# Gate and up products of a 512-token SwiGLU half step by seven half-size products, their weight sums and part of adaLN on GpSimd

## The chip, the cores and the metric

The kernel runs on one NeuronCore of a Trainium2 chip. The metric is device time in microseconds for one launch. In the profile the engines are PE (TensorE, with its weight loads as PEld), DVE (VectorE), ACT (ScalarE), POOL (GpSimd) and SP (SyncE, which issues most DMAs). SBUF is the on-chip memory and PSUM the accumulators that PE writes.

## The reference

Two transformer layers over 256 latent and 256 context tokens, 1024 features, everything in float32. Each layer has a SwiGLU half step, a token mixer with four kinds of attention, and a second SwiGLU half step; all three start from an RMS norm whose scale and shift (and the gate of the result) come from adaLN, a product of a condition vector with `w_ada`. Latent and context tokens have different condition vectors. In the last layer only latent tokens go past the mixer. Cut to the part that matters here:

```python
for l in range(2):
    mod   = (silu(c)     @ w_ada[l] + b_ada[l]).reshape(B, 9, 1, D)   # latent
    mod_c = (silu(c_ctx) @ w_ada[l] + b_ada[l]).reshape(9, D)         # context
    h  = h  + 0.5 * mod[:, 2] * swiglu(modulate(h,  norm_ffn1[l], mod[:, 0], mod[:, 1]), w_gu, w_down)
    hc = hc + 0.5 * mod_c[2]  * swiglu(modulate(hc, norm_ffn1[l], mod_c[0], mod_c[1]), w_gu, w_down)
    ...  # token mixer
    h  = h + 0.5 * mod[:, 8] * swiglu(...)          # and hc in the first layer only
# swiglu(u) = (silu(u @ w_gate) * (u @ w_up)) @ w_down, w_gate and w_up 1024 x 2816
```

## The kernel before

Activations lie feature-major: a tile has 128 features on the partitions and up to 512 tokens along it, tokens 0 to 255 latent (`LAT`), 256 to 511 context (`CTX`). Every float32 operand of a large product is split into a high part in the PE's fast format (`fp32r`) and the rest (`lo`): ACT casts the high part (L127), DVE subtracts it from the raw tile (L128), and `mm3` (L132) issues three matmuls, high x high, high x low and low x high. A weight block is 128 x 1024 (8 contraction tiles `k` of 128 x 128), DMA'd by SP into one of three raw buffers (`wraw`) and split into one of five `whi`/`wlo` pairs (`weights`, L119).

A half step is `ffn` (L350). Its 22 tiles of 128 hidden features come in chunks of 8, 8 and 6 (`FF_CHUNKS`). For a tile j, `pair(j)` (L375) loads and splits a gate block and an up block, 2 x 8 x 3 matmuls of 512 columns sum into two PSUM banks, and `activate` (L353) takes silu of gate on ACT, multiplies by up on DVE (L358) and splits the result into `ah`/`al` (L371, L372). After a chunk the eight down tiles follow: for output tile m, 8 (or 6) x 3 matmuls over the chunk's activations, and DVE adds the result with its gate into the residual stream `h` (L336). The last five down tiles of a half step run for one half of the tokens after the other (matmuls of 256 columns), woven with the next norm. The first two tiles of a half step are done k by k behind the norm that makes `u`, the normed operand (`first_products`, L264, or `first_opening`, L987, in the first half step). The second half step of layer 2 has 256 tokens only.

adaLN's vectors other than the first two are computed beside the half steps: `Jobs` (L315) hands out tiles at a fixed rate, `jobs.run(2)` after a gate/up tile and `jobs.run(1)` after a down tile. A tile (`ada_tile`, L292) is a 128 x 1024 block of `w_ada` DMA'd into `wa`, and two DVE instructions (L298) that multiply it with the latent and the context condition vector and add up along the row. The first half step has 48 such tiles, the second 32, the third (layer 2, first) 48.

The code is written in the order of the data flow. A planner with its own estimates of the instructions' costs orders each engine's queue from it and places every wait; `keep_in_program_order` fixes single instructions (here adaLN's products and the opening's matmuls). On the chip each engine takes its queue in order.

Of the kernel before, what the change touches and what calls it, by code (L numbers as in the profile page):

```python
# [49 lines left out]
def body(nc, tc, es, a):  # L50
# [47 lines left out]
    def late_constants():  # L98
        """-lam per layer, on every partition; rev"""
# [31 lines left out]

    def mm3(ps, lw, rw, start, stop, pin=False):  # L132
        (lh, ll), (rh, rl) = lw, rw
        ins = nc.tensor.matmul(ps, lh, rh, start=start, stop=False)  # L134
        if pin:
            tc.keep_in_program_order(ins)
        nc.tensor.matmul(ps, lh, rl, start=False, stop=False)  # L137
        nc.tensor.matmul(ps, ll, rh, start=False, stop=stop)  # L138
# [1062 lines left out]
```

## Time and profile before

| what | value |
|---|---|
| timed runs, median (lowest to highest) | 2156.77 us (2156.07 to 2157.89) |
| profiled execution, span from first to last instruction | 2153.2 us |
| PE busy | 2107.4 us (98%) |
| DVE busy | 1469.2 us (68%) |
| ACT busy | 911.8 us (42%) |
| POOL busy | 180.7 us (8%) |
| mean granted PE clock (1 is 2.4 GHz) | 0.997 |

For the profiled execution the page gives the span; the timed runs are 3.6 us above it in the median. Busy time is the share of the span in which an engine works on an instruction. A record of a DVE or POOL instruction runs from its start to its end and includes any time in which it is held inside; two instructions in a row on an engine overlap by a little, so what one costs in a dense stretch is read from start to start. Matmuls overlap more: 512 columns are recorded with 0.39 us but follow each other at a shorter distance.

### The profile page before, as it was taken

How to read it: one execution, taken by the hardware profiler on the slowest of the kernel's cores; microseconds unless marked ns; L12 is line 12 of the kernel's file. 1: busy time of each engine (PE TensorE's matmuls, PEld its weight loads, DVE VectorE, ACT ScalarE, POOL GpSimd, SP SyncE). 2: the span in 40 equal slices, each digit the busy share in tenths (PEclk: the TensorE clock that was granted, in tenths of full speed). 3: DMA queues.
4: the chain of work that ended last, by engine and by line, in shares of the span. 5: the costliest groups of instructions: out<-in, count | busy, mean ns of one | idle time of the engine just before them, and what ended most of it. 6: DMA issues, size and time to landing. Idle time of an engine off the chain costs nothing.

```text
span 2153.2 us, 31572 instructions
## 1 busy us (share of the span) xinstructions
PE 2107.4 (98%) x12130; PEld 1805.8 (84%) x12130; DVE 1469.2 (68%) x2639; ACT 911.8 (42%) x1456; POOL 180.7 (8%) x322
## 2 busy tenths in 40 slices
PE   7999999999999999999999999999999999999998
PEld 5888888987777877988888898888889888999998
DVE  6776767678767665566665558767667887787655
ACT  3422222467655563432222233222225776765443
POOL 0000000110012112100000010000002433120000
PEclk9999999999999999999999999999999999999999
DMA  8555554241232223245444336555542335355553
GB/s 331 173 178 178 177 176 150 69 121 47 66 100 73 88 66 118 92 157 156 140 154 150 105 118 203 179 176 186 165 127 90 105 106 138 128 168 171 192 183 102
DMA packets 95207, 301.52 MB, mean 140 GB/s; under 512 B 18640, under 2 KB 20048, under 8 KB 94672
## 3 DMA queue, kind: packets, MB, share of 16 engines
q1 hardware_dynamic: 92080, 295.10, 43.0%
q0 software_dynamic: 2688, 4.20, 1.0%
q8 instruction: 96, 1.57, 0.3%
q14 instruction: 55, 0.45, 0.1%
q10 hardware_dynamic: 288, 0.20, 0.0%
HBM read 294.21 MB, written 1.05 MB: 137 GB/s over the span
## 4 chain that ended last, share of the span: by engine, by line
PE 89%; DVE 5%; ACT 2%; issue 1%; POOL 1%; DMA 1%; SPq 0%; DVEq 0%; POOLq 0%; ACTq 0%
PE pgu L134 13%; PE pgu L137 13%; PE pgu L138 13%; PE pd L137 6%; PE pd L138 6%; PE pd L134 6%; PE pgt L134 4%; PE pgt L137 4%; PE pgt L138 4%; PE av L789 2%; PE pj L134 2%; PE pj L137 2%; PE pj L138 2%; PE psS L735 2%; PE tps L775 1%
## 5 line engine op out<-in xcount | busy, mean ns | idle before, releaser
L127 ACT CAST whi<-wraw 128x1024 fp32r<-128x1024 f32 (+2 forms) x414 | 423.1, 1024 | 993.8 <-PE pgu L137 434.7
L128 DVE TENSOR_TENSOR wlo<-wraw,whi 128x1024 fp32r<-128x1024 f32 (+2 forms) x414 | 495.2, 1197 | 160.6 <-ACT whi L127 141.5
L134 PE MATMUL pgu<-uh,whi 128*128 128x512 f32 (+1 forms) x1440 | 511.9, 357 | 1.4 <-ACT sg L357 0.9
L137 PE MATMUL pgu<-ul,whi 128*128 128x512 f32 (+1 forms) x1440 | 512.7, 356 | 0.6 <-DVE ul L230 0.4
L138 PE MATMUL pgu<-uh,wlo 128*128 128x512 f32 (+1 forms) x1440 | 512.2, 356 | 0.0
L298 DVE SCALAR_TENSOR_TENSOR junk<-wa,sbc 128x1024 f32<-128x1024 f32 x256 | 312.3, 1220 | 3.1
L134 PEld LDWEIGHTS pgu<-uh,whi 128*128 128x128 f32 x1440 | 271.1, 189 | 43.4 <-issue 2.5
L137 PEld LDWEIGHTS pgu<-ul,whi 128*128 128x128 f32 x1440 | 272.1, 189 | 39.4 <-DVE ul L230 1.1
L138 PEld LDWEIGHTS pgu<-uh,wlo 128*128 128x128 f32 x1440 | 272.1, 189 | 39.1 <-DVE wlo L128 0.3
L137 PE MATMUL pd<-al,whi 128*128 128x512 f32 (+1 forms) x794 | 273.4, 344 | 0.2 <-DVE al L372 0.2
L134 PE MATMUL pd<-ah,whi 128*128 128x512 f32 (+1 forms) x794 | 273.5, 345 | 0.0
L138 PE MATMUL pd<-ah,wlo 128*128 128x512 f32 (+1 forms) x794 | 273.1, 344 | 0.0
L134 PE MATMUL pgt<-uh,whi 128*128 128x512 f32 (+1 forms) x512 | 176.5, 345 | 0.4 <-ACT cacc L548 0.4
L358 DVE TENSOR_TENSOR af<-sg,pgu 128x512 f32<-128x512 f32 (+1 forms) x86 | 53.6, 625 | 179.5 <-PE pgu L138 179.5
L137 PE MATMUL pgt<-ul,whi 128*128 128x512 f32 (+1 forms) x512 | 174.1, 340 | 0.0
L138 PE MATMUL pgt<-uh,wlo 128*128 128x512 f32 (+1 forms) x512 | 173.8, 339 | 0.0
L137 PEld LDWEIGHTS pd<-al,whi 128*128 128x128 f32 x794 | 149.3, 188 | 20.9 <-DVE al L372 0.9
L134 PEld LDWEIGHTS pd<-ah,whi 128*128 128x128 f32 x794 | 149.2, 188 | 20.0
L138 PEld LDWEIGHTS pd<-ah,wlo 128*128 128x128 f32 x794 | 149.1, 188 | 19.9
L336 DVE SCALAR_TENSOR_TENSOR h<-pd,mod,h 128x256 f32<-128x256 f32 x168 | 76.4, 480 | 105.7 <-PE pd L138 105.3
L148 POOL TENSOR_TENSOR rq<-ry 128x2 f32<-128x2 f32 (+2 forms) x48 | 12.1, 252 | 1252.5 <-DVE ry L146 1241.6
L134 PEld LDWEIGHTS pgt<-uh,whi 128*128 128x128 f32 x512 | 97.6, 191 | 13.2 <-issue 3.3
(240 smaller groups left out, 3125.2 us busy)
## 6 DMA issues: line engine op xcount, KB each, us to landing
wraw<-wgu SPq DMA_DIRECT2D x176, 512.0 KB, 3.3
wa<-wada SPq DMA_DIRECT2D x128, 512.0 KB, 4.2
wraw<-wd SPq DMA_DIRECT2D x64, 512.0 KB, 3.6
wraw<-wgate SPq DMA_DIRECT2D x64, 512.0 KB, 3.3
wraw<-win SPq DMA_DIRECT2D x28, 512.0 KB, 3.3
wraw<-wd SPq DMA_DIRECT2D x32, 384.0 KB, 3.1
w<-wada SPq DMA_DIRECT2D x16, 512.0 KB, 8.0
wraw<-wbr SPq DMA_DIRECT2D x16, 512.0 KB, 3.3
```

The costliest lines, as they stand in the source:

```text
L127: nc.scalar.copy(hi[:, :n], raw[:, :n])
L128: nc.vector.tensor_sub(lo[:, :n], raw[:, :n], hi[:, :n])
L134: ins = nc.tensor.matmul(ps, lh, rh, start=start, stop=False)
L137: nc.tensor.matmul(ps, lh, rl, start=False, stop=False)
L138: nc.tensor.matmul(ps, ll, rh, start=False, stop=stop)
L148: eng.tensor_mul(q[:, :n], y[:, :n], y[:, :n])
L298: ins = nc.vector.scalar_tensor_tensor(junk, w, 1.0, sbc[:, v], op0=ALU.mult, op1=ALU.mult, accum_out=m[:, t, v:v + 1])
L336: nc.vector.scalar_tensor_tensor(h[k][:, hv[0]:hv[1]], ps[:, off:off + S], gate[:, k, v:v + 1], h[k][:, hv[0]:hv[1]], op0=ALU.mult, op1=AL ...
L358: nc.vector.tensor_mul(af[:, :ntok], sg[:, :ntok], pu[:, :ntok])
L735: nc.tensor.matmul(ps[:, :nk], q_[:, q0:q0 + P], k_[:, self.k0:T], start=z == 0, stop=z == len(qs) - 1 and not bias_mm)
L775: nc.tensor.transpose(tps[:, b], self.p[:, b * P:(b + 1) * P], ident)
L789: nc.tensor.matmul(av[un.qt * 64:(un.qt + 1) * 64], V[br](u0.k0 // P + b, hd), un.pT[:, b], start=b == 0, stop=b == kt - 1)
```

## The change

The gate/up products of the tiles j from 3 on (from 4 on in the first half step) in the three half steps with 512 tokens are done by one level of Strassen's scheme in Winograd's form. The 2 x 2 block matrix of weights is (gate, up) by (k 0 to 3, k 4 to 7), that of the operand is (k 0 to 3, k 4 to 7) by (latent, context). Seven products of 4 x 3 matmuls with 256 columns take the place of eight. `combine` forms the operand's sums T1 to T4 once per half step (each split again into high and low; T4 overwrites the context half of `u`), beside the last plain tile. `seven(j)` forms four weight sums of 128 x 512 per tile on GpSimd, partly in place in the raw tiles, splits the results (`x2`, `x3`, `x1`, beside `xg`, the gate block itself), and adds the products up with five DVE sums of 256 columns. adaLN's context product moves to GpSimd (`tensor_mul` into the `wa` tile), its row sum to ACT one step later; tiles of which only the latent vector is used (layer 2, from vector 5 on) have one product. The rates of `Jobs`, some buffer counts (a fourth raw buffer for odd j, `ah`/`al` 8 for 10, `af` 2 for 3) and tags change. Comments of the code are dropped as well. The core of the diff:

```diff
-    def weights(src, shape):
-        """load a [128, k, cols] block of a weight and split it"""
+    def load(src, shape, pool=None):
         n = shape[1] * shape[2]
-        raw = wp.tile([P, 1024], F32, name="wraw", tag="wraw", bufs=3)
-        rv = raw[:, :n].rearrange("p (k c) -> p k c", k=shape[1])
-        nc.sync.dma_start(rv, src)
+        raw = (pool or wp).tile([P, 1024], F32, name="wraw", tag="wraw", bufs=1 if pool else 3)
+        nc.sync.dma_start(raw[:, :n].rearrange("p (k c) -> p k c", k=shape[1]), src)
+        return raw[:, :n]
+    def split(raw, k):
+        n = raw.shape[1]
         hi = wp.tile([P, 1024], F32R, name="whi", tag="whi")
         lo = wp.tile([P, 1024], F32R, name="wlo", tag="wlo")
-        nc.scalar.copy(hi[:, :n], raw[:, :n])
-        nc.vector.tensor_sub(lo[:, :n], raw[:, :n], hi[:, :n])
-        return (hi[:, :n].rearrange("p (k c) -> p k c", k=shape[1]),
-                lo[:, :n].rearrange("p (k c) -> p k c", k=shape[1]))
-    def mm3(ps, lw, rw, start, stop, pin=False):
+        nc.scalar.copy(hi[:, :n], raw)
+        nc.vector.tensor_sub(lo[:, :n], raw, hi[:, :n])
+        return (hi[:, :n].rearrange("p (k c) -> p k c", k=k), lo[:, :n].rearrange("p (k c) -> p k c", k=k))
+    def weights(src, shape):
+        return split(load(src, shape), shape[1])
...
+    def ada_vectors(l, i):
+        return 1 if l == DEPTH - 1 and i > 4 else 2
-        for v in range(2):
-            junk = pool.tile([P, D], F32, name="junk", tag="junk", bufs=1)
-            ins = nc.vector.scalar_tensor_tensor(junk, w, 1.0, sbc[:, v], op0=ALU.mult, op1=ALU.mult, accum_out=m[:, t, v:v + 1])
-            if pin:
-                tc.keep_in_program_order(ins)
+        junk = pool.tile([P, D], F32, name="junk", tag="junk", bufs=1)
+        ins = nc.vector.scalar_tensor_tensor(junk, w, 1.0, sbc[:, 0], op0=ALU.mult, op1=ALU.mult, accum_out=m[:, t, 0:1])
+        if pin:
+            tc.keep_in_program_order(ins)
+        if ada_vectors(l, i) == 1:
+            return None
+        nc.gpsimd.tensor_mul(w, w, sbc[:, 1])
+        def total():
+            tc.keep_in_program_order(nc.scalar.activation(w, w, AF.Copy, accum_out=m[:, t, 1:2]))
+        return total
...
+        def __init__(self, todo, pool, steps):
+            self.todo, self.rate, self.due, self.pool = todo, len(todo) / steps, 0.0, pool
+            self.sbc, self.n, self.behind = None, 0, []
+            self.need = KD if todo and todo[0][1] in (2, 8) else 0
+        def first(self, n):
+            while self.n < n and self.todo:
+                self.run(0 if self.due >= 1 else 1 / self.rate)
+        def settle(self):
+            for f in self.behind:
+                f()
+            self.behind = []
+        def run(self, steps):
+            self.due += steps * self.rate
+            self.settle()
...
-                ada_tile(l, i, t, self.pool, self.sbc, self.n < PIN)
+                total = ada_tile(l, i, t, self.pool, self.sbc, self.n < PIN)
                 self.n += 1
                 if t == KD - 1:
+                    self.settle()
+                    if total is not None:
+                        total()
                     ada_end(l, i)
+                elif total is not None:
+                    self.behind.append(total)
...
-    W0 = [("w0", 4)] * 4 + [("wa", 2)] * 2 + [("junk", 1)]
+    W0 = [("T", 6)] * 6 + [("junk", 1)]
+    STEP_PLAIN, STEP_SEVEN, STEP_DOWN, STEPS = 2.0, 1.0, 1.6, 49
...
-            af = fp.tile([P, T], F32, name="af", tag="af", bufs=3)
+            af = fp.tile([P, T], F32, name="af", tag="af", bufs=2)
...
-            ah = fp.tile([P, T], F32R, name="ah", tag="ah", bufs=10)
-            al = fp.tile([P, T], F32R, name="al", tag="al", bufs=10)
+            return split_act(af)
+        def split_act(af):
+            ah = fp.tile([P, T], F32R, name="ah", tag="ah", bufs=8)
+            al = fp.tile([P, T], F32R, name="al", tag="al", bufs=8)
...
+        HK = KD // 2
+        B = {}
+        def combine():
+            def whole(r, hv, tag, bufs):
+                f = fp.tile([P, HK, S], F32, name="f", tag=tag, bufs=bufs)
+                for k in range(HK):
+                    h_, l_ = uk(u, r * HK + k, *hv)
+                    nc.gpsimd.tensor_add(f[:, k], h_.bitcast(F32), l_.bitcast(F32))
+                return f
+            def halves_of(f):
+                th, tl = [fp.tile([P, HK, S], F32R, name="T", tag="T", bufs=6) for _ in range(2)]
+                nc.scalar.copy(th, f)
+                nc.vector.tensor_sub(tl, f, th)
+                return [(th[:, k], tl[:, k]) for k in range(HK)]
+            f12, t1 = whole(0, CTX, "wa", 2), whole(0, LAT, "junk", 1)
+            nc.gpsimd.tensor_sub(t1, f12, t1)
+            t2 = whole(1, CTX, "wa", 2)
+            nc.gpsimd.tensor_sub(f12, t2, f12)
+            nc.vector.tensor_sub(t2, t2, t1)
+            B["T2"], B["T3"], B["T1"] = halves_of(t2), halves_of(f12), halves_of(t1)
+            t4 = whole(1, LAT, "junk", 1)
+            nc.vector.tensor_sub(t4, t4, t2)
+            def last():
+                for k in range(HK):
+                    h_, l_ = uk(u, k, *CTX)
+                    nc.scalar.copy(h_, t4[:, k])
+                    nc.vector.tensor_sub(l_, t4[:, k], h_)
+            B["T4"] = [uk(u, k, *CTX) for k in range(HK)]
+            B["11"] = [uk(u, k, *LAT) for k in range(HK)]
+            B["21"], B["22"] = [[uk(u, HK + k, *hv) for k in range(HK)] for hv in (LAT, CTX)]
+            return last
+        def seven(j):
+            g, v = [load(a[wgu][l, j, e], [P, KD, P], fp if (2 * j + e) % 4 == 3 else None) for e in range(2)]
+            n = HK * P
+            a11, a12, a21, a22 = g[:, :n], g[:, n:], v[:, :n], v[:, n:]
+            xg = split(g, KD)
+            s3 = fp.tile([P, n], F32, name="s3", tag="s3", bufs=1)
+            nc.gpsimd.tensor_sub(s3, a11, a21)
+            nc.gpsimd.tensor_add(a21, a21, a22)
+            nc.gpsimd.tensor_sub(a11, a21, a11)
+            nc.gpsimd.tensor_sub(a12, a12, a11)
+            x2 = split(g, KD)
+            x3 = split(s3, HK)
+            x1 = split(v, KD)
+            def product(ps, w_, z, b, start=True):
+                for k in range(HK):
+                    mm3(ps[:, :S], wk(w_, z * HK + k), B[b][k], start and k == 0, k == HK - 1, more=not start)
+            pa, pb, pc, pd_ = [psmm.tile([P, 512], F32, name=f"p7{z}", tag="mm") for z in "abcd"]
+            sg = fp.tile([P, T], F32, name="sg", tag="sg", bufs=2)
+            af = fp.tile([P, T], F32, name="af", tag="af", bufs=2)
+            u2 = fp.tile([P, S], F32, name="u2", tag="u2", bufs=1)
+            u3 = fp.tile([P, S], F32, name="u3", tag="u3", bufs=1)
+            product(pa, xg, 0, "11")
+            nc.scalar.copy(u2, pa[:, :S])
+            product(pb, x2, 0, "T2")
+            nc.vector.tensor_add(u2, u2, pb[:, :S])
+            product(pa, xg, 1, "21", False)
+            nc.scalar.activation(sg[:, :S], pa[:, :S], AF.Silu)
+            product(pc, x3, 0, "T3")
+            nc.vector.tensor_add(u3, u2, pc[:, :S])
+            product(pd_, x1, 0, "T1")
+            nc.vector.tensor_add(af[:, S:], u3, pd_[:, :S])
+            product(pc, x1, 1, "T4", False)
+            nc.vector.tensor_add(af[:, :S], u2, pc[:, :S])
+            product(pd_, x2, 1, "22", False)
+            nc.vector.tensor_add(sg[:, S:], u2, pd_[:, :S])
+            nc.scalar.activation(sg[:, S:], sg[:, S:], AF.Silu)
+            nc.vector.tensor_mul(af, sg, af)
+            return split_act(af)
...
+        nplain = 3 if opening is None else 4
...
+                if len(halves) > 1 and j >= nplain:
+                    act.append(seven(j))
+                    jobs.run(STEP_SEVEN)
+                    continue
...
+                if j == nplain - 1 and len(halves) > 1:
+                    jobs.settle()
+                    last_sum = combine()
...
+                if j == nplain - 1 and len(halves) > 1:
+                    last_sum()
-                jobs.run(2)
+                jobs.run(STEP_PLAIN)
...
+            if c == 0:
+                jobs.first(jobs.need)
...
-                jobs.run(1)
+                jobs.run(STEP_DOWN)
```

## Rows read from the trace of the kernel before

**Rows 1.** The page's head: span, busy time, share and instructions of each engine.
```profile
span 2153.2 us, 31572 instructions
PE 2107.4 (98%) x12130; PEld 1805.8 (84%) x12130; DVE 1469.2 (68%) x2639; ACT 911.8 (42%) x1456; POOL 180.7 (8%) x322
```
**Rows 2.** Windows: length, busy us (instructions) by engine, PE clock, DMA share, GB/s.
```profile
96.00:390.00 294.00, 294.00 (x1340) 243.31 (x1338) 208.27 (x325) 76.33 (x99) 0.00 (x0) 1.00 0.53 168
...
925.00:1258.00 333.00, 333.00 (x1513) 275.69 (x1512) 198.89 (x295) 90.68 (x116) 0.00 (x0) 1.00 0.46 144
...
1295.00:1628.00 333.00, 333.00 (x1512) 275.64 (x1511) 236.12 (x362) 90.75 (x116) 0.00 (x0) 1.00 0.53 169
```
**Rows 3.** Timeline (start us, us, engine, line, operation), PE: 512 columns, first and 55th.
```profile
199.66 0.39 PE L134 MATMUL pgu<-uh,whi 128*128 128x512 f32 x1
...
211.90 0.39 PE L134 MATMUL pgu<-uh,whi 128*128 128x512 f32 x1
```
**Rows 4.** Timeline, PE and PEld: 256 columns, first and 51st; a weight load.
```profile
2000.02 0.28 PE L137 MATMUL pd<-al,whi 128*128 128x256 f32 x1
...
2005.95 0.28 PE L134 MATMUL pd<-ah,whi 128*128 128x256 f32 x1
...
2000.02 0.19 PEld L138 LDWEIGHTS pd<-ah,wlo 128*128 128x128 f32 x1
```
**Rows 5.** Timeline, DVE: instructions that follow each other at once; last, with a PSUM input.
```profile
178.96 1.23 DVE L128 TENSOR_TENSOR wlo<-wraw,whi 128x1024 fp32r<-128x1024 f32 x1
180.10 0.68 DVE L372 TENSOR_TENSOR al<-af,ah 128x512 fp32r<-128x512 f32 x1
180.71 1.22 DVE L298 SCALAR_TENSOR_TENSOR junk<-wa,sbc 128x1024 f32<-128x1024 f32 x1
181.85 0.08 DVE L298 DVE_READ_ACCUMULATOR junk<-wa,sbc 128x1 f32 x1
...
1923.92 1.08 DVE L528 TENSOR_TENSOR sig<-pbr,sig 128x256 f32<-128x256 f32 x3
```
**Rows 6.** Timeline, POOL: two sums in a row with no DVE instruction in their way.
```profile
744.41 2.54 POOL L529 TENSOR_TENSOR merged<-merged,sig 128x512 f32<-128x512 f32 x2 [26.13 <-DVE sig L528]
...
1910.76 1.44 POOL L529 TENSOR_TENSOR merged<-merged,sig 128x256 f32<-128x256 f32 x2 [8.08 <-DVE sig L528]
```
**Rows 7.** Groups by line, ACT: busy us, mean ns | idle before, releasers.
```profile
L127 ACT CAST whi<-wraw 128x1024 fp32r<-128x1024 f32 x364 | 382.0, 1051 | 878.0 <-PE pgu L137 370.8 <-PE pd L137 254.8 <-PE pgt L137 93.1
```
**Rows 8.** Timeline, POOL and DVE, where both work: near 390, 852 and 1899.
```profile
390.72 1.23 DVE L128 TENSOR_TENSOR wlo<-wraw,whi 128x1024 fp32r<-128x1024 f32 x1 [0.21 <-ACT whi L127]
390.87 1.13 POOL L153 TENSOR_TENSOR rq<-rq,rv 128x2 f32<-128x2 f32 x1
...
852.45 3.83 POOL L529 TENSOR_TENSOR merged<-merged,sig 128x512 f32<-128x512 f32 x2 [1.29 <-DVE sig L528]
852.83 0.68 DVE L528 TENSOR_TENSOR sig<-pbr,sig 128x512 f32<-128x512 f32 x1
853.43 1.71 DVE L128 TENSOR_TENSOR wlo<-wraw,whi 128x1024 fp32r<-128x1024 f32 x1
855.06 2.59 DVE L927 TENSOR_TENSOR ml<-merged,mh 128x512 fp32r<-128x512 f32 x2
...
1899.18 1.22 DVE L128 TENSOR_TENSOR wlo<-wraw,whi 128x1024 fp32r<-128x1024 f32 x1
1899.40 3.27 POOL L529 TENSOR_TENSOR merged<-merged,sig 128x256 f32<-128x256 f32 x2 [5.02 <-DVE sig L528]
1900.64 1.44 DVE L128 TENSOR_TENSOR wlo<-wraw,whi 128x1024 fp32r<-128x1024 f32 x1
```
**Rows 9.** Timeline, DVE: end of u, and the third pair's product, second half step.
```profile
916.66 0.88 DVE L230 SCALAR_TENSOR_TENSOR ul<-nt,mod,uh 128x256 fp32r<-128x256 f32 x2 [0.19 <-ACT uh L229]
...
935.60 0.69 DVE L358 TENSOR_TENSOR af<-sg,pgu 128x512 f32<-128x512 f32 x1 [0.18 <-PE pgu L138]
```
**Rows 10.** Timeline, DVE: the opening's sums of squares.
```profile
8.19 4.67 DVE L1026 TENSOR_TENSOR acc<-acc,sq 128x512 f32<-128x512 f32 x6 [1.82 <-ACT sq L1024]
```

More of the change, by code (lines that the diff above doesn't have):

```diff
@@ L116, in late_constants, with mm3 @@
         nc.scalar.copy(rev, raw)
[L119 removed]
+    def load(src, shape, pool=None):
         n = shape[1] * shape[2]
[L122 to L124 removed]
+        raw = (pool or wp).tile([P, 1024], F32, name="wraw", tag="wraw", bufs=1 if pool else 3)
[3 more added lines that the diff above has]
+        n = raw.shape[1]
         hi = wp.tile([P, 1024], F32R, name="whi", tag="whi")
         lo = wp.tile([P, 1024], F32R, name="wlo", tag="wlo")
[L127 to L132 removed]
+        nc.scalar.copy(hi[:, :n], raw)
[3 more added lines that the diff above has]
+        return split(load(src, shape), shape[1])
+    def mm3(ps, lw, rw, start, stop, pin=False, more=False):
         (lh, ll), (rh, rl) = lw, rw
[L134 removed]
+        ins = nc.tensor.matmul(ps, lh, rh, start=start, stop=False, skip_group_check=more)
         if pin:
             tc.keep_in_program_order(ins)
[L137 to L138 removed]
+        nc.tensor.matmul(ps, lh, rl, start=False, stop=False, skip_group_check=more)
+        nc.tensor.matmul(ps, ll, rh, start=False, stop=stop, skip_group_check=more)
     def rsqrt_cols(ps, n, inv, eps, eng):
@@ L315, in body @@
     class Jobs:
-        def __init__(self, todo, pool, slots=56):
-            self.todo, self.rate, self.due, self.pool = todo, len(todo) / slots, 0.0, pool
-            self.sbc, self.n = None, 0
-        def run(self, slots):
-            self.due += slots * self.rate
+        def __init__(self, todo, pool, steps):
[12 more added lines that the diff above has]
+            self.settle()
             while self.todo and self.due >= 1:
@@ L404, in ffn @@
                 act.append(activate(g[0][1], g[1][1]))
-                jobs.run(2)
+                if j == nplain - 1 and len(halves) > 1:
+                    last_sum()
+                jobs.run(STEP_PLAIN)
             nk = j1 - j0
+            if c == 0:
+                jobs.first(jobs.need)
             last = c == len(FF_CHUNKS) - 1
@@ L987, in first_opening @@
     def first_opening(nrm, weights_of, fp):
-        st = fp.tile([P, KD, 32], F32, name="st", tag="st", bufs=1)
+        st = fp.tile([P, KD, 32], F32, name="st", tag="u3", bufs=1)
         nc.vector.memset(st, 0.0)
@@ L1014, in ada_finish @@
             nc.vector.tensor_scalar(A[:, f], A[:, f], gains[:, 0, f:f + 1], None, op0=ALU.mult)
-        acc = fp.tile([P, T], F32, name="acc0", tag="af", bufs=3)
-        rs = fp.tile([P, T], F32, name="rs", tag="rs", bufs=1)
+        acc = fp.tile([P, T], F32, name="acc0", tag="af", bufs=2)
+        rs = fp.tile([P, T], F32, name="rs", tag="s3", bufs=1)
         y, pairs = [], {}
@@ L1022, in squares @@
                 nc.sync.dma_start(h[k], a["hT"][k])
-                sq = acc if k == 0 else fp.tile([P, T], F32, name="sq0", tag="af", bufs=3)
+                sq = acc if k == 0 else fp.tile([P, T], F32, name="sq0", tag="af", bufs=2)
                 nc.scalar.activation(sq, h[k], AF.Square)
@@ L1034, in rows, with pair_of @@
                 nrm.ps[lo, hi] = rs[:, lo:hi]
-        def load(j):
+        def pair_of(j):
             pairs[j] = [(w_, psmm.tile([P, 512], F32, name="pgu", tag="mm")) for w_ in weights_of(j)]
@@ L1045, in products @@
                 mm3(p_, wk(w_, k), uk(nrm.u, k, 0, T), k == 0, k == KD - 1, True)
-        do = {"H": squares, "C": cols, "R": rows, "P": ada_products, "F": ada_finish, "W": load, "S": step, "M": products}
+        do = {"H": squares, "C": cols, "R": rows, "P": ada_products, "F": ada_finish, "W": pair_of, "S": step, "M": products}
         for op in OPENING.split():
@@ L1061, in body @@
         with tc.tile_pool(name=f"f1_{l}", bufs=1, reuse_waits="tile") as fp:
-            jobs, opening = Jobs(ada_jobs(0, range(2, 8)) if l == 0 else ada_jobs(1, range(3, NMOD)), fp), None
+            jobs, opening = Jobs(ada_jobs(0, range(2, 8)) if l == 0 else ada_jobs(1, range(3, NMOD)), fp, STEPS), None
             if l == 0:
@@ L1079, in body @@
         with tc.tile_pool(name=f"f2_{l}", bufs=1, reuse_waits="tile") as fp:
-            jobs, nxt = Jobs([] if last else ada_jobs(0, [8]) + ada_jobs(1, range(3)), fp), None
+            jobs, nxt = Jobs([] if last else ada_jobs(0, [8]) + ada_jobs(1, range(3)), fp, STEPS), None
             if not last:
```

2 lines of the change are left out of this document (added).

## The prediction

> **What bounds the kernel now.** I read the page's totals first: TensorE (PE) is busy 98% of the 2153.2 us span, VectorE (DVE) 68%, GpSimd (POOL) 8% [rows 1]. Then the stretches: in the gate/up and down stages of the three half steps with 512 tokens PE is busy every microsecond, at the full granted clock (2.4 GHz), while GpSimd does nothing [rows 2]. So there the kernel is bound by matmul columns, and only two things can move the time: fewer PE microseconds, or another engine that becomes slower than PE. The timed runs have a median of 2156.77 us, 3.6 us above the profiled span; I add differences worked out in the profile to that median.
>
> **PE's part.** Matmuls of 512 columns start 54 in 12.24 us, 0.2267 us each [rows 3]; those of 256 columns start 50 in 5.93 us, 0.1186 us each, although each brings its own weight load [rows 4]. A pair of tiles (gate and up tile j) costs 2 x 8 x 3 = 48 wide matmuls, 10.88 us. seven(j) has 7 x 4 x 3 = 84 of 256 columns: 9.96 us. That is 0.92 us less, not an eighth, because each start carries about 0.013 us beside its columns. The first three tiles of a half step (four in the first) stay plain, so 18 + 19 + 19 = 56 tiles become sevens: 51.5 us off PE. The last half step has 256 tokens and is untouched.
>
> The Trainium skill, "TensorE: Matmul & The Clock Gate", section "Back-to-back issue gap", gives N / 2.4 GHz plus 2.5 ns for a start, so by that page 512 columns take 0.2158 us, 256 take 0.1092, and the 56 tiles would give back 66 us (estimate). The rows show some 12 ns where it has 2.5; the measured gap decides.
>
> **What the split tiles add on DVE and GpSimd, for one seven.** In a dense stretch DVE starts the next instruction 1.14 us after a 1024-wide split, and 0.61 us after a 512-wide one [rows 5]. The four splits (xg, x2, x1 of 1024, x3 of 512) take 3 x 1.14 + 0.61 = 4.03; the product sg x af and the split al 0.61 each: 5.25 us of instructions with two inputs in SBUF. Five sums of 256 with one input in PSUM follow, 1.08 / 3 = 0.36 each [rows 5]: 1.8 us. GpSimd alone takes 2.54 / 2 = 1.27 us for a 512-wide sum and 1.44 / 2 = 0.72 for 256 [rows 6], so 0.00215 us a column; four weight sums are 5.08 us, and adaLN's 1024-wide product is 1.27 + 512 x 0.00215 = 2.37 us (no such row, hence this line). Taken engine by engine all this fits beneath 9.96 us: DVE 7.05 plus 1.22 for an adaLN tile, GpSimd 5.08 + 2.37. ACT's 3.5 casts of 1.05 and smaller work of some 3 us fit too [rows 7].
>
> **But the two engines do not run side by side.** It shows three times [rows 8]. A two-column GpSimd product beside a split at 390.72 lasts 1.13 us and ends with the split, at 392.0. Between 852.45 and 857.65 GpSimd's two sums (2.54 alone) and DVE's 1024 split and two 512 splits (1.14 + 1.22 alone) take 5.20 us; 4.90 is their plain sum, and had they run together it would be 2.54. Both engines' records are stretched (3.83, 1.71, 2.59) because each waits inside them for the other. The product at 852.83, with one input in PSUM, keeps its 0.68 us meanwhile. So GpSimd's reads of SBUF and DVE instructions with two SBUF inputs take turns, and what counts is their sum. Near 1899 four such instructions take 3.49 us against a plain sum of 3.72 (2 x 1.14 + 2 x 0.72): handing over can save 6%.
>
> The Trainium skill has this rule in "SBUF — State Buffer", section "Who interferes with whom": one port pair, held for the whole instruction, so the other side blocks fully. By it the plain sums below would hold in full; the 3.49 us say a little less, and the low end of my range takes that.
>
> **The turn-taking sum per stage.** One seven: 5.25 + 5.08 = 10.33 us, already more than PE's 9.96. An adaLN tile adds 1.14 on DVE and 2.37 on GpSimd = 3.51 (before: two DVE products, 2.28). Tiles come by jobs.run at todo / 49 a step, one step behind a seven.
> - First half step (48 tiles, 0.98 a step): 10.33 + 0.98 x 3.51 = 13.77 against 10.88 before: +2.89 x 18 = +52.0.
> - Second (32 tiles, 0.653): 12.62, +1.74 x 19 = +33.1.
> - Third: 16 tiles have two vectors, the rest one: 5 sevens at 13.77, 14 at 10.33 + 0.98 x 1.14 = 11.45: +14.5 + 8.0 = +22.5.
> Together +107.6. The down tiles: 24 matmuls of 512 are 5.44 us; 1.6 steps bring 1.57 x 3.51 + 1.14 = 6.65 us while the tiles last, +1.21 for 16 in the first half step and 4 in the third: +24. In the second 1.045 x 3.51 + 1.14 = 4.81 fits.
>
> **combine().** Sixteen 256-wide sums (11.5), two 1024-wide (4.7), five 1024-wide DVE instructions (5.7) and four 256-wide (1.4): 23.3 us of turns. u is complete at about 917.5 in the second half step, the third pair ends at 935.6 [rows 9]: an 18 us window, in which four weight splits (4.6), two al (1.2) and 2.6 adaLN tiles (9.1) want 15 us of turns too. Product T2 is the second of the first seven and needs the end of that chain. The overhang is 23.3 + 15 - 18 = 20 us if everything queues in order, 0 if the sums of the early half go ahead; I take 10, three times: +30 (0 to 60).
>
> **Edits that cost little.** The fourth raw buffer, ah/al at 8 instead of 10 (a chunk holds 8 at most) and the u3/s3 tags: nothing, as a chunk's first act is needed only after the downs have let go. af at 2 buffers makes the opening's squares take turns with their adds (six adds in 4.67 us now [rows 10]): +1, 0 to 3. ACT's totals (1024 wide, about a cast) are behind, one step late: nothing. SP's queue: a raw load waits until x1 or x2 of two tiles earlier is split, and adaLN's loads stand behind it; it is late with the sevens, not on its own. What waits where: a DVE split held by GpSimd has the PSUM sums queued behind it, and a later product reuses their bank, so the stall reaches PE within the seven.
>
> **Sum.** +107.6 + 24 + 30 + 1 = +163: 2156.8 + 163 = 2319 us. Low end: turns spread evenly over sevens and downs, no combine overhang. First half step: 48 x 3.51 + 18 x 10.33 + 23.3 + 36 of plain and down splits = 414, less 6% = 389, against 337 of PE before (20 pairs and the downs): +52. The other two then hide (377 x 0.94 = 354 against 359 before). About 2205. High end: DVE's five PSUM sums find no turn of GpSimd's to hide in, 56 x 1.8 = +101, and combine at 20 each, less a little of both: 2440.
>
> **Rivals.**
> - *PE stays the bound (the other side).* If GpSimd's 5.08 us and DVE's 5.25 overlap, PE sets the pace and the 51.5 us come out: 2105. It decides where the real turns in a seven stay below 9.96. For it: each engine alone is below that. Against it: every overlap in [rows 8].
> - *Turns bind, but are evened out.* The low end, 2160 to 2205: the sevens run on ahead while adaLN's GpSimd products move into the downs. Against: there is room for about one tile ahead (five whi buffers, four a tile).
> - *DVE in order is worse than the sum.* PE waits for a split, DVE for a PE product, GpSimd for DVE: above 2440. For it: the sums sit in one queue with the next tile's splits.
> - *Narrow matmuls wait for weight loads.* A load takes 0.19 us, 84 of them 16 us a tile: +5 x 56, about 2440. Against: in [rows 4] loads take 0.19 and matmuls, each with its own, still start every 0.119 us. Nearly excluded.
>
> The Trainium skill, "Perfetto Trace Analysis", section "Identifying the Most-Contended Engine", judges PE by load time, which would speak for the last rival; the trace bears it out only as long as loads do not overlap, and here they do.
>
> **Chances.** Forecast 2205 to 2440: 0.73. Evened out, 2161 to 2205: 0.06. Above 2440, by order or loads: 0.03. Within 0.2% (2152 to 2161, about what a measurement can tell from none): 0.04. PE-bound, faster: 0.14. So slower 0.82. Range 2155 to 2440 leaves out the faster case and the tail above; the forecast's own range is 2205 to 2440.
>
> **What would show it.** Right: in a half step's sevens POOL's 512-wide sums average well over 1.27 us and the wlo splits over 1.23, both at once; the first matmuls of two sevens lie about 13.8, 12.6 and 11.5 us apart; PE idles there behind wlo and the u sums. PE steps: 84 matmuls per seven, 0.119 us apart where they run. Downs of the first half step about 6.6 us apart. Wrong: sums at 1.3 us beside splits at 1.2 in the same microseconds, and sevens 10 us apart. A granted clock below the 1.00 of [rows 2] in the sevens would add a cost that I did not price.

## The result, and the profile after

The changed kernel takes 2440.02 us (median of 4 runs, 2436.35 to 2440.96) against 2157.33 (2156.07 to 2158.11) for the kernel before, which has one run more here than in the table ahead of the prediction: a ratio of 1.131, 95% interval 1.129 to 1.132. It is slower, by the mechanism of the forecast, and by 283 us where the forecast had 163: it lies on the upper end of the range, 2440, with runs on either side of it.

The page's head, against [rows 1]: PE's busy time has not fallen (2107 before), although its matmuls have fewer columns, and its share has gone from 98% to 88%.

```profile
span 2434.6 us, 36967 instructions
PE 2138.3 (88%) x14146; PEld 1916.9 (79%) x14146; DVE 1778.1 (73%) x2806; ACT 1142.1 (47%) x1893; POOL 843.1 (35%) x696
```

Where the 281 us of span are is read from PE's timeline, as the distance from the first matmul of one stretch to the first of the next (us; the downs' third stretch is the one that ends in the next phase):

| half step | gate/up before | gate/up after | downs before | downs after |
|---|---|---|---|---|
| first | 96.3, 87.1, 65.3 | 133.6, 137.3, 95.6 | 44.8, 44.8, 36.7 | 44.5, 44.2, 36.6 |
| second | 90.7, 87.0, 65.3 | 128.8, 111.2, 85.8 | 44.8, 44.8, 37.0 | 44.6, 45.8, 36.8 |
| third | 91.2, 87.0, 65.3 | 143.8, 107.5, 71.0 | 44.8, 44.8, 35.6 | 45.5, 45.1, 35.6 |

The gate/up stretches hold +279.5 (118, 83 and 79), the downs 0.6; the rest, 1 us, lies outside the three half steps. The windows of four stretches of sevens (the second and third of half step 1, the second of 2 and of 3) and of one of downs, in the columns of [rows 2], where PE was busy every microsecond at clock 1.00 before:

```profile
160.30:204.80 44.50, 44.43 (x193) 35.63 (x192) 31.73 (x40) 14.98 (x22) 24.75 (x11) 1.00 0.53 173
204.80:342.10 137.30, 95.33 (x676) 91.14 (x675) 115.01 (x124) 58.58 (x94) 85.88 (x44) 0.86 0.39 124
386.30:482.00 95.70, 68.11 (x506) 65.87 (x505) 82.54 (x90) 42.12 (x68) 62.56 (x31) 0.88 0.41 126
1190.90:1302.10 111.20, 87.59 (x673) 84.80 (x672) 92.93 (x106) 49.80 (x77) 66.40 (x36) 0.94 0.38 117
1659.80:1767.30 107.50, 86.56 (x673) 84.63 (x672) 85.61 (x118) 41.65 (x62) 41.51 (x28) 0.92 0.49 154
```

In the 137.3 us of eight sevens DVE and GpSimd are "busy" 115 and 86: 201 together, which by itself would speak against turns. But a record also counts the time in which an instruction is blocked, as the timeline shows (start, duration; DVE's and GpSimd's rows near 264 and 282):

```profile
263.11 2.30 DVE L308 SCALAR_TENSOR_TENSOR junk<-wa,sbc 128x1024 f32<-128x1024 f32 x1
265.34 0.41 DVE L483 TENSOR_TENSOR u<-u,p7b 128x256 f32<-128x256 f32 x1
...
280.17 2.31 DVE L308 SCALAR_TENSOR_TENSOR junk<-wa,sbc 128x1024 f32<-128x1024 f32 x1
282.41 0.41 DVE L487 TENSOR_TENSOR u<-u,p7c 128x256 f32<-128x256 f32 x1
282.74 3.29 DVE L131 TENSOR_TENSOR wlo<-wraw,whi 128x1024 fp32r<-128x1024 f32 x1
```
```profile
264.40 2.13 POOL L465 TENSOR_TENSOR wraw<-wraw 128x512 f32<-128x512 f32 x1
266.50 2.35 POOL L313 TENSOR_TENSOR wa<-wa,sbc 128x1024 f32<-128x1024 f32 x1
...
279.77 1.62 POOL L465 TENSOR_TENSOR wraw<-wraw 128x512 f32<-128x512 f32 x1
282.56 2.38 POOL L313 TENSOR_TENSOR wa<-wa,sbc 128x1024 f32<-128x1024 f32 x1 [1.17 <-DVE junk L308]
```

At 282.56 GpSimd's product takes its 2.38 us alone; the split that DVE starts at 282.74 ends at 286.03, 1.1 us after the product: it stood for 2.2 us and then ran its 1.14. At 264.40 it is the other way: the sum of 1.27 us stands until DVE's product is through at 265.41 and ends 1.1 us later, 2.13 in all. The sum u at 282.41, with one input in PSUM, keeps 0.41 us. The groups (busy us, mean ns) say the same over the whole span: what was 1.27 us alone [rows 6] averages 1.47 to 1.73, the 1024-wide split of 1.23 [rows 5] 1.46, adaLN's DVE product 1.78 (1.22 before); the sums with a PSUM input average 0.41, what they also take beside a running GpSimd sum (265.34 above).

```profile
L313 POOL TENSOR_TENSOR wa<-wa,sbc 128x1024 f32<-128x1024 f32 x96 | 253.4, 2640 | 241.7 <-DVE junk L308 186.9 <-ACT wa L316 33.7 <-ACT whi L130 17.1
L463 POOL TENSOR_TENSOR wraw<-wraw 128x512 f32<-128x512 f32 x56 | 96.8, 1728 | 4.3
L462 POOL TENSOR_TENSOR s<-wraw 128x512 f32<-128x512 f32 x56 | 82.3, 1469 | 173.3 <-DVE wlo L131 94.8 <-DMA wa<-wada 37.3 <-DMA wraw<-wgu 29.5
```
```profile
L131 DVE TENSOR_TENSOR wlo<-wraw,whi 128x1024 fp32r<-128x1024 f32 x420 | 611.2, 1456 | 181.5 <-ACT whi L130 161.9 <-PE pgu L143 12.5 <-PE p7d L144 4.5
L308 DVE SCALAR_TENSOR_TENSOR junk<-wa,sbc 128x1024 f32<-128x1024 f32 x128 | 227.2, 1775 | 32.4 <-DMA wa<-wada 32.1
L487 DVE TENSOR_TENSOR u<-u,p7c 128x256 f32<-128x256 f32 x56 | 23.1, 413 | 1.6 <-PE p7c L144 1.4
```

The waits (engine and line waiting, for whom: us, times, longest) close the circle: GpSimd waits for DVE's split of the same raw weights before it may overwrite them, ACT's cast waits for GpSimd's last sum, and PE for a sum that stands in DVE's queue behind blocked splits.

```profile
ACT whi L130 <- POOL wraw L465: 147.3, 52, 15.1
POOL wraw L464 <- DVE wlo L131: 146.0, 46, 17.4
...
PE p7c L140 <- DVE u L487: 78.7, 39, 6.0
```

PE's own step came out as forecast: 60 narrow matmuls in a row, first and last, start 7.03 us apart, 0.1192 each ([rows 4] had 0.1186).

```profile
1849.86 0.28 PE L140 MATMUL p7a<-uh,whi 128*128 128x256 f32 x1
...
1856.89 0.28 PE L144 MATMUL p7d<-T,wlo 128*128 128x256 f32 x1
```

And combine() in the second half step, where [rows 9] promised an 18 us window: DVE's last part of u, GpSimd, PE.

```profile
1035.13 0.88 DVE L236 SCALAR_TENSOR_TENSOR ul<-nt,mod,uh 128x256 fp32r<-128x256 f32 x2 [0.19 <-ACT uh L235]
```
```profile
1045.91 1.68 POOL L464 TENSOR_TENSOR wraw<-wraw 128x512 f32<-128x512 f32 x1 [17.36 <-DVE wlo L131]
...
1053.80 3.27 POOL L313 TENSOR_TENSOR wa<-wa,sbc 128x1024 f32<-128x1024 f32 x1 [1.17 <-DVE junk L308]
1057.03 7.99 POOL L426 TENSOR_TENSOR f<-uh,ul 128x256 f32<-128x256 f32 x8
...
1072.44 2.34 POOL L438 TENSOR_TENSOR f<-f 128x1024 f32<-128x1024 f32 x1
```
```profile
1060.86 0.58 PE L140 MATMUL p7a<-uh,whi 128*128 128x256 f32 x1 [5.47 <-ACT u L481]
1078.21 0.58 PE L140 MATMUL p7b<-T,whi 128*128 128x256 f32 x1 [14.41 <-ACT T L431]
```

u is complete at 1036.0, but GpSimd's queue holds the first seven's weight sums and two adaLN products first, and combine's first sum starts at 1057.0. The window is gone; PE stands 5.5 us before p7a's second product, for a copy in ACT's queue, and 14.4 before p7b, for T2.

### The profile page after: what moved, and what is told of

Same layout as the page of the kernel before. It is cut to its first block, busy times and chain, and to the rows that moved or that the text cites. A ratio compares the mean times of both kernels' runs of the same rounds, so it can differ in the third digit from the quotient of the medians.

```text
span 2434.6 us, 36967 instructions
## 1 busy us (share of the span) xinstructions
PE 2138.3 (88%) x14146; PEld 1916.9 (79%) x14146; DVE 1778.1 (73%) x2806; ACT 1142.1 (47%) x1893; POOL 843.1 (35%) x696
## 5 line engine op out<-in xcount | busy, mean ns | idle before, releaser
L131 DVE TENSOR_TENSOR wlo<-wraw,whi 128x1024 fp32r<-128x1024 f32 (+1 forms) x470 | 663.1, 1412 | 205.2 <-ACT whi L130 185.0
L130 ACT CAST whi<-wraw 128x1024 fp32r<-128x1024 f32 (+1 forms) x470 | 480.2, 1024 | 679.0 <-POOL wraw L465 147.3
L313 POOL TENSOR_TENSOR wa<-wa,sbc 128x1024 f32<-128x1024 f32 x96 | 253.4, 2640 | 241.7 <-DVE junk L308 186.9
L308 DVE SCALAR_TENSOR_TENSOR junk<-wa,sbc 128x1024 f32<-128x1024 f32 x128 | 227.2, 1775 | 32.4 <-DMA wa<-wada 32.1
L140 PE MATMUL p7a<-uh,whi 128*128 128x256 f32 x448 | 136.7, 305 | 64.0 <-ACT u L481 63.0
L316 ACT ACTIVATE wa<-wa 128x1024 f32<-128x1024 f32 x96 | 101.6, 1058 | 194.1 <-POOL wa L313 194.1
L140 PE MATMUL pgu<-uh,whi 128*128 128x256 f32 (+1 forms) x544 | 164.3, 306 | 1.4 <-ACT sg L395 0.9
L143 PE MATMUL pgu<-ul,whi 128*128 128x256 f32 (+1 forms) x544 | 164.9, 304 | 0.4 <-DVE ul L236 0.4
L144 PE MATMUL pgu<-uh,wlo 128*128 128x256 f32 (+1 forms) x544 | 164.3, 303 | 0.0
L140 PEld LDWEIGHTS p7a<-uh,whi 128*128 128x128 f32 x448 | 93.7, 209 | 67.6 <-ACT u L481 65.6
```

Of the source, the lines that this page charges most:

```text
L130: nc.scalar.copy(hi[:, :n], raw)
L131: nc.vector.tensor_sub(lo[:, :n], raw, hi[:, :n])
L140: ins = nc.tensor.matmul(ps, lh, rh, start=start, stop=False, skip_group_check=more)
L143: nc.tensor.matmul(ps, lh, rl, start=False, stop=False, skip_group_check=more)
L144: nc.tensor.matmul(ps, ll, rh, start=False, stop=stop, skip_group_check=more)
L308: ins = nc.vector.scalar_tensor_tensor(junk, w, 1.0, sbc[:, 0], op0=ALU.mult, op1=ALU.mult, accum_out=m[:, t, 0:1])
```

## The experiments

The theory: DVE instructions with two SBUF inputs and GpSimd's instructions take turns, and the sum of turns sets the sevens. Rivals: GpSimd's own length; DVE's queue order and latency; the new work on ACT. The kernel before was run beside each (2154 to 2156 us, so up to 3 us below its time above). e9 and e12 have four runs, the others one; differences are to 2440.0, and those of a few us mean nothing, as four runs of a changed kernel lie 4 to 6 us apart.

**e1, adaLN's product back on DVE.**
```diff
-        nc.gpsimd.tensor_mul(w, w, sbc[:, 1])     (and its total on ACT)
+        nc.vector.scalar_tensor_tensor(junk, w, 1.0, sbc[:, 1], ..., accum_out=m[:, t, 1:2])
```


> adaLN's context product goes back to DVE; the weight sums stay on GpSimd. Taking turns (GpSimd's reads of SBUF and DVE's two-SBUF instructions add up): 96 products of 2.37 us on GpSimd become 96 of 1.14 on DVE, so turns fall by 118 us in all, 73 of them in the stretches of sevens (59 tiles run there); 2320 to 2365 us. Rival, DVE alone is the bound: it gets 1.22 us more per tile, so slower than 2440. Rival, GpSimd alone is too slow: it loses 250 of its 640 us of busy time and the sevens come near to PE's pace, under 2260.

2350.65 us: -89, as the turns said. DVE got more work and the kernel became faster, so DVE's load alone is not the bound.

**e2, the weight sums back on DVE.**
```diff
-            nc.gpsimd.tensor_sub(s3, a11, a21)    (and the other three)
+            nc.vector.tensor_sub(s3, a11, a21)
```


> The four weight sums go to DVE; adaLN's context product stays on GpSimd. Taking turns: a sum costs 0.61 instead of 1.27, a seven 7.69 + 3.51 per adaLN tile, 148 us less in 56 sevens, and more of adaLN fits into the down tiles: 2230 to 2300 us. Rival, DVE alone is the bound: 7.05 + 2.44 + 1.22 = 10.7 us per seven, slower or equal to the changed kernel's 2440 only if DVE was the bound there; if it becomes the bound now, 2190 to 2230. Rival, the narrow products themselves cost the time: no change from 2440.

2367.16: -73, right in sign, but 67 above the expected range.

**e3, no weight sums** (left out, so the products use unsummed weights).
```diff
-            nc.gpsimd.tensor_sub(s3, a11, a21)    (and the other three)
```


> The four weight sums are left out (x2, x1 and x3 are split from the raw blocks, so the products are of other numbers); all splits, products, the operand's sums and adaLN on GpSimd stay. Taking turns: a seven has 5.25 + 3.51 per adaLN tile = 8.7 us of turns, below PE's 9.96, so sevens run at about 10 us and what stays is combine's stall (15 to 25 us, three times) less 51 us of PE: 2150 to 2180 us. Rival, narrow matmuls or the scheme's PSUM sums cost the time: over 2300.

2283.0: -157, between the two. The last stretch of the third half step, where no adaLN product is left for GpSimd, took 60.5 us for six sevens, PE's 59.8: there the sevens run at PE's pace. The time is still 103 us above the expected range: the middle stretch of the second half step takes 93.2 us for eight sevens, though PE needs 79.7 and the turns left in it add up to 65 (8 x 5.25, 6 DVE and 7 GpSimd products). Below PE's time the plain sum of turns does not say what a seven takes.

**e4, no sevens** (plain pairs; adaLN's product stays on GpSimd).
```diff
-        nplain = 3 if opening is None else 4
+        nplain = 99
```


> All tiles stay plain pairs (no sevens, no combine); adaLN's context product stays on GpSimd with its rates. Taking turns: a pair has 2.9 us of splits and two adaLN tiles of 3.51, 9.8 us against PE's 10.88, the down tiles of the first chunk 6.65 against 5.44: 2157 to 2175 us. Rival, adaLN on GpSimd makes most of the loss by itself: over 2250.

2203.87: above what I expected. Moving adaLN's product alone costs 47 us, in one pair stretch (100.1 for 87.1) and two of downs (63.2 and 60.9 for 44.8). In the downs PE waited for act's last tile, whose product af stood in DVE's queue behind two adaLN products, the first of which had waited 2.6 us for its load; GpSimd's products of these two tiles then hold the split and al that follow, to 2.8 us each (DVE, then POOL, then PE):

```profile
270.74 1.23 DVE L308 SCALAR_TENSOR_TENSOR junk<-wa,sbc 128x1024 f32<-128x1024 f32 x1 [2.62 <-DMA wa<-wada]
...
272.10 1.22 DVE L308 SCALAR_TENSOR_TENSOR junk<-wa,sbc 128x1024 f32<-128x1024 f32 x1
...
273.25 0.68 DVE L396 TENSOR_TENSOR af<-sg,pgu 128x512 f32<-128x512 f32 x1
273.85 2.77 DVE L131 TENSOR_TENSOR wlo<-wraw,whi 128x1024 fp32r<-128x1024 f32 x1
276.54 2.82 DVE L413 TENSOR_TENSOR al<-af,ah 128x512 fp32r<-128x512 f32 x1
```
```profile
272.11 6.71 POOL L313 TENSOR_TENSOR wa<-wa,sbc 128x1024 f32<-128x1024 f32 x2 [7.37 <-DMA wa<-wada]
```
```profile
279.42 0.79 PE L143 MATMUL pd<-al,whi 128*128 128x512 f32 x1 [4.29 <-DVE al L413]
```

That load is issued when a buffer of the two comes free, now after three engines have used it. e11 below tests this.

**e5, sums replaced by write-only work** (each sum becomes three memsets of its output, 0.526 us each, so GpSimd is as long at it as before; the sums' values are lost).
```diff
-            nc.gpsimd.tensor_sub(s3, a11, a21)    (and the other three)
+            nc.gpsimd.memset(s3, 0.01 * j + 0.01) (three times each)
```


> Each of the four weight sums on GpSimd becomes three memsets of the same tile (it only writes, and reads nothing from SBUF; the weights of the products are constants then). The chain cast, split, GpSimd, cast, split keeps its order and GpSimd keeps its work, about 1.3 us a sum by the 0.2 us for 128 columns in the trace; only the turns with DVE's two-SBUF instructions go. Taking turns: close to the run without sums (2283 us), 2260 to 2310. Rival, GpSimd's slow link in the chain makes the loss, whoever holds SBUF: 2400 to 2440.

2308.06: -132 of the 157 that leaving the sums out gave. GpSimd's time at the sums is no less (1.58 us each for 1.27); what is gone are its reads. All 672 fills last 0.51 to 0.54 us: none is held by DVE, though 173 of them lie wholly within the record of a two-input DVE instruction (split, product or al). The groups of this run, against those of after above:

```profile
L466 POOL MEMSET wraw<- 128x512 f32 x56 | 29.5, 527 | 2.5
```
```profile
L308 DVE SCALAR_TENSOR_TENSOR junk<-wa,sbc 128x1024 f32<-128x1024 f32 x128 | 164.5, 1285 | 42.0 <-DMA wa<-wada 41.6
L131 DVE TENSOR_TENSOR wlo<-wraw,whi 128x1024 fp32r<-128x1024 f32 x420 | 607.3, 1447 | 162.9 <-ACT whi L130 160.6
```

adaLN's DVE product is back at 1.29 us, from 1.78. The splits stay at 1.45, as adaLN's GpSimd products still read; in e8, without those, they are at 1.24. The Trainium skill, "SBUF — State Buffer", section "Who interferes with whom", says just this: DVE instructions with two SBUF inputs contend with GpSimd instructions that read SBUF, not with those that only write it. The run agrees.

**e6, no totals** (adaLN's row sums on ACT left out).
```diff
-            tc.keep_in_program_order(nc.scalar.activation(w, w, AF.Copy, accum_out=m[:, t, 1:2]))
```


> ACT's row sum behind each GpSimd product of adaLN is left out (the context vectors are constants then); all GpSimd and DVE work stays. Turns stay as they are: 2410 to 2440 us. Rival, ACT's queue: the sum stands in ACT's queue waiting for GpSimd (194 us of ACT's idle time in the changed kernel), with the casts of the next weights behind it: 2300 to 2380 us.

2431.55: -8.5 by one run, -5 if each is set against the kernel before beside it, hardly above the spread. ACT's totals are not it.

**e7, no combine** (T1, T2, T3 are slices of u; T4 not computed).
```diff
-            f12, t1 = whole(0, CTX, "wa", 2), whole(0, LAT, "junk", 1)   (to T1 and last())
+            B["T2"], B["T3"], B["T1"] = [[uk(u, HK + k, *hv) ...] for hv in (LAT, CTX, LAT)]
```


> The operand's sums T1 to T4 are left out (those products read halves of u instead); the sevens, weight sums and adaLN stay. combine's 23.3 us of turns per half step all exposed: 3 x 23 = 70 us less, 2360 to 2375. As forecast, 10 exposed in each: 2405 to 2415. Rival, a chain that is longer than its turns (GpSimd's 16 sums one after the other, ACT's casts): over 100 us less, under 2340.

2367.54: -72.5, 24 a half step, in the first gate/up stretch of each alone (110.7, 108.2, 116.6 for 133.6, 128.8, 143.8). That is as much as all 23.3 us of combine's turns; whether they stand there as turns or as one chain of instructions, this run does not tell apart.

**e8, sums and adaLN on DVE** (both edits of e1 and e2; combine stays on GpSimd).

> Weight sums and adaLN's context product both on DVE; only combine uses GpSimd. No turns are left in the sevens: DVE itself has 9.49 us per seven and 2.44 per adaLN tile (1.22 with one vector), 11.9, 11.1 and 10.7 to 11.9 us in the three half steps, against 10.88 of a plain pair: +24 us, some 20 more where adaLN tiles of the down stage run into the sevens, and combine's stall of 15 to 25 us three times: 2220 to 2280 us. Rival, DVE is worse loaded than before without GpSimd's help, as the change assumes: over 2440. Rival, the scheme itself costs the time: over 2300.

2269.38: -171, as expected, and about what e1 and e2 give together (162).

**e9, DVE does it all, with adaLN's tiles kept apart from the sevens** (e8, combine on DVE too, spread over three plain pairs; adaLN issued in pairs and downs only; 37 sevens).
```diff
-        nplain = 3 if opening is None else 4
+        nplain = 16 if opening is not None else 8 if l == 0 else 5
-    STEP_PLAIN, STEP_SEVEN, STEP_DOWN, STEPS = 2.0, 1.0, 1.6, 49
+    STEP_PLAIN, STEP_SEVEN, STEP_DOWN = 3.6, 0.0, 3.1     (counted in vectors)
```


> Everything that the change gave GpSimd goes to DVE (weight sums, adaLN's second product, combine's sums), adaLN's tiles come only in plain pairs and downs, combine is spread over three plain pairs, and fewer tiles become sevens (j from 16 in the first half step, from 8 in the second, from 5 in the third: 37 in all). A seven then has 5.25 + 4 x 0.61 + 5 x 0.36 = 9.49 us of DVE against 9.96 of PE, and no turns with GpSimd. If PE can be kept fed at that load, 37 x 0.92 = 34 us come out, less what combine and the seams leave open (0 to 15): 2120 to 2140. Rival, order on DVE: the run with all of it on DVE spent 63.2 us on six sevens that had little adaLN (10.5 each); then 37 x (10.5 - 10.88) = -13 and combine's 15 us partly open three times: 2140 to 2180. A time above 2200 would say that the sevens can't be fed by DVE alone either.

2176.58 (2173.11 to 2179.24), ratio 1.010, interval 1.008 to 1.011: the upper end of the rival. A stretch of six sevens, in the stretch of eight before it the first matmul of product T3 in two successive sevens, and ACT's queue just before the second:

```profile
1171.10:1234.00 62.90, 61.22 (x493) 59.30 (x492) 56.81 (x91) 27.90 (x45) 0.00 (x0) 1.00 0.30 92
```
```profile
1064.25 0.39 PE L140 MATMUL p7c<-T,whi 128*128 128x256 f32 x1 [0.18 <-ACT whi L130]
...
1074.92 0.39 PE L140 MATMUL p7c<-T,whi 128*128 128x256 f32 x1 [0.20 <-ACT whi L130]
...
1075.58 0.28 PE L140 MATMUL p7b<-T,whi 128*128 128x256 f32 x1
```
```profile
1073.00 1.05 ACT L130 CAST whi<-wraw 128x1024 fp32r<-128x1024 f32 x1 [5.00 <-DVE wraw L465]
...
1074.27 0.60 ACT L130 CAST whi<-s 128x512 fp32r<-128x512 f32 x1
```

Without GpSimd and at full clock the sevens come every 10.67 us once a stretch runs, where PE alone needs 9.96 and a pair 10.88. DVE is busy for 56.8 of 62.9 us (9.5 a seven). In this seven PE stops once, at T3: its cast (1074.27) stands in ACT's queue behind one that has waited 5 us for DVE's last weight sum (L465). The first matmul there comes 0.36 us late (the one before it starts at 1074.45), and the next three starts, to 1075.58, are 0.22 apart in place of 0.119: together the 0.7 us. Of the 0.92 us that PE would give back, 0.2 are left, and the seams take those: the five stretches that are all sevens take 375.9 us for 34, 11.06 each.

**e10, adaLN issued in pairs and downs only** (engines as in the change).
```diff
-    STEP_PLAIN, STEP_SEVEN, STEP_DOWN, STEPS = 2.0, 1.0, 1.6, 49
+    STEP_PLAIN, STEP_SEVEN, STEP_DOWN, STEPS = 2.0, 0.0, 1.6, 31
```


> The changed kernel with adaLN's tiles issued in plain pairs and downs only (a step of a seven counts 0, and 31 steps for 49): the engines are as in the change. Turns theory: sevens without tiles come back to about 10.5 us (56 of them, 588 for some 797 measured in their stretches), and downs with 2.5 two-vector tiles take 1.14 + 2.48 x 3.51 = 9.8 for 5.44 in the first half step, 6.9 in the second, and 9.8 for some 7 in the third: +84, +28, +28. In all 2440 - 209 + 140 = 2370 if the tiles run where they are issued, and down to 2290 where downs hide what PE leaves. Rival: tiles slide from the downs into the sevens that follow, as they did in the changed kernel, and nothing is won: 2410 to 2440.

2485.64: worse than both. The tiles did not move. Windows with `junk` alone (two instructions a tile) of the second stretch of sevens and the downs behind it, first after, then this run:

```profile
204.80:342.10 137.30, 26.06 (x28) 0.86 0.39 124
342.10:386.30 44.20, 14.46 (x16) 1.00 0.50 158
```
```profile
205.40:348.40 143.00, 23.22 (x28) 0.83 0.39 126
348.40:393.10 44.70, 14.56 (x16) 1.00 0.45 149
```

14 tiles in the eight sevens and 8 in the eight downs, in both, and no other stretch of the three half steps differs by more than two: DVE's queue has one two-vector tile to a down tile here, although more are issued. (In e9, with both products on DVE, eight downs of the first half step hold 10 to 12.) Why this run is 46 us slower with the same placement stays open.

**e11, e4 with three buffers for adaLN's tiles.**
```diff
-        w = pool.tile([P, D], F32, name="wa", tag="wa", bufs=2)
+        w = pool.tile([P, D], F32, name="wa", tag="wa", bufs=3)
```


> No sevens (plain pairs), adaLN's second product on GpSimd, as in the run that took 2203.9, but with three buffers for adaLN's tiles in place of two. If the 47 us of that run are the wait for a tile's buffer (a load stands until the tile's total on ACT is done, adaLN's product on DVE waits for the load, and the pair's product af is queued behind it on DVE), the third buffer takes most of it: 2160 to 2180. Rival, the products' turns themselves: no change, 2195 to 2210.

2165.21: 39 of the 47 us are gone, with the same products on the same engines. The wait of adaLN's DVE product for its load, first e4, then this run:

```profile
DVE junk L308 <- DMA wa<-wada: 69.6, 49, 3.3
```
```profile
DVE junk L308 <- DMA wa<-wada: 18.3, 9, 3.4
```

So without sevens most of the cost of adaLN's edit comes from a buffer held too long; turns add to it behind a late load, as the rows of e4 show, and with the loads in time at most 9 us are left for them. A third buffer was not tried with the sevens; e6, which frees the buffer a total earlier, suggests that there it is the smaller part.

**e12, e9 with al on GpSimd.**
```diff
-                nc.vector.tensor_sub(al, af, ah)
+                nc.gpsimd.tensor_sub(al, af, ah)       (in sevens)
```


> The kernel of the run before with everything on DVE (37 sevens, 411 us in their stretches, 11.1 each), with one instruction of a seven on GpSimd again: al = af - ah, 512 wide, which nothing needs before the downs. DVE falls from 9.49 to 8.88 us a seven; turns are 4.64 + 2.44 + 1.27 = 8.35, both below PE's 9.96. Turns theory: GpSimd costs nothing while the sum of turns stays below PE, and DVE's relief shows: sevens of 10.2 to 10.8, 2145 to 2165. Rival, any GpSimd instruction between DVE's costs more than its turn, since DVE's queue stops behind it: 1.27 - 0.61 = 0.66 more a seven or worse, 2195 to 2230.

2186.29 (2183.66 to 2187.93), ratio 1.014, interval 1.012 to 1.016: between the two expectations, and 9.7 above e9. Turns below PE's time are not free: where DVE's queue is nearly full (90% in e9's stretch), GpSimd's turn is taken from it, even for an instruction that only the downs need. GpSimd's al takes 1.73 us in the mean, and DVE's sum s beside it 1.10, for 0.68 in e9. No version with sevens beat the kernel before.

## Why the prediction was right, and where its sizes were off

**Right.** The bound moved from PE to the turns of DVE and GpSimd, in the sevens. That is shown by e5 (same GpSimd time, no reads), by the stretched records, and fits the sum: the nine stretches of sevens take 885.7 us in all, and what the trace has in them is 56 x 10.33 us of sevens' turns, 70 DVE and 54 GpSimd products of adaLN (70 x 1.14 + 54 x 2.37) and three times combine's 23.3: 578 + 208 + 70 = 856 us, 97% of the time. The rival that PE stays the bound falls with the same rows; the one that narrow matmuls wait for their loads falls with PE's 0.1192 us. By this sum DVE's queue order can be no more than the remaining 3%. The sum serves where turns exceed PE's time, as here; in e3's second half step and in e12, where they don't, time is lost all the same.

**Too small, combine: +30 forecast, 72.5 by e7.** I wrote that it overhangs 20 us "if everything queues in order, 0 if the sums of the early half go ahead", and took 10. Measured are 24 a half step, above even the 60 us that the term allowed in all. Everything queued in order: GpSimd had the first seven's sums and adaLN's products ahead of it, and the plain pair's time went by unused. That is +40.

**In the wrong place, adaLN's tiles: +24 in the downs forecast, 0.6 measured.** I counted them where jobs.run issues them: "Downs of the first half step about 6.6 us apart". They are 5.5 apart, with one tile each where a tile has two vectors. The rest ran in the sevens, where nothing hides them: in the first half step 29 (5, 14 and 10) where 17.6 were counted, in all nine stretches 208 us of adaLN turns for some 138. That is +70 there and -24 (the downs' share). The "first matmuls of two sevens" show it: in the middle stretches 17.2, 13.9 and 13.4 us in the mean for my 13.8, 12.6 and 11.5.

**The sum again.** 163 + 40 + 70 - 24 = 249 of 281. What is left, 32, is 0.6 us a seven that the plain sum of turns has no term for; its cause stays open. e9 has such a gap too: a seven every 10.67 us for 9.49 of DVE and 9.96 of PE. That the time lies on the range's upper end is luck: 2440 stood there mainly for DVE's five PSUM sums finding no turn to hide in (1.8 us a seven, +101), of which at most the 0.6 can be seen; the excess came from combine and adaLN's tiles.

**At nothing, wrongly: "ACT's totals ... behind, one step late: nothing".** ACT's time is indeed nothing (e6), but a tile now holds its buffer through DVE, GpSimd and ACT, the next load waits for it on SP, and DVE's product for the load, with the pair's af behind it. Where I named what is queued behind a waiting DVE split, I did not ask it of adaLN's product. With plain pairs this wait costs 39 us (e4, e11). It is also why my expectation for e4 was too low; for e2 and e3 I take it to play a part, but did not test it.

**A page read too simply.** The section that I cite for a matmul's start, "Back-to-back issue gap" in the Trainium skill's "TensorE: Matmul & The Clock Gate", gives that formula for a single matmul by itself, and 131 ns at 512 columns for a stream with weight loads. I left that out. The 0.2267 us measured here [rows 3] lie above both; the sum uses these.

**Not priced: the clock.** I had named it. In the nine stretches of sevens the granted clock is 0.78 to 0.98 in the mean, with PE idle in between, and PE's busy time grows (95.3 us for eight sevens that need 79.7 at full clock, in a stretch of 137.3). As PE waits there anyway, it is not shown to cost anything; no run separates it.

## What to carry to other kernels

Before moving DVE work to GpSimd, add up the two engines' instructions that read SBUF (DVE's with two inputs there) as if one engine did them, and compare that sum with the bound. A sum below the bound is no promise: in e12, with DVE 90% busy, one 512-wide GpSimd subtraction a tile still cost time. Where the work added comes in tiles that a planner places, count them in the engine's queue of the trace, not where the loop issues them; and for each buffer ask how many engines now hold it before the next load can start. A chain that must end before the first new product (combine) gets no overlap for free: look at what stands ahead of it on its engine.

## What the runs showed of the hardware that was not expected

- A GpSimd fill of 128x512 takes 0.526 us, is not held by DVE's two-input instructions, and leaves DVE's products at 1.29 us (e5); a GpSimd sum of the same size takes 1.27 us and, with the adaLN products on GpSimd, had them at 1.78.
- A GpSimd product of 128x1024 takes 2.33 us at the shortest of its 96 records in the changed kernel and 2.40 in the median, as the 2.37 worked out from [rows 6].
- In e9 a seven with 9.49 us of DVE's instructions and 9.96 of PE's ran at 10.67, with DVE busy 90% and PE 97% of a stretch: these two nearly full engines, which wait for each other and for ACT, did not reach the longer one's time. In the seven looked at, one stop of 0.36 us cost PE 0.7, as the next three matmuls came 0.22 us apart.
